# Where the selection rounds, the norm, the bias table and the clearing of S stand in a gated hybrid block

## The chip, the cores and the metric

The kernel runs on one core of a Trainium2 chip. The metric is device time in microseconds (us) of one execution. The kernel before takes 1400.65 us (median of three runs, 1398.86 to 1402.32).

Five instruction streams run side by side on the core: TensorE (PE, matrix multiplies), VectorE (DVE), ScalarE (ACT), GpSimd (POOL) and SyncE (SP, which issues the DMAs here). Each executes its own instructions in the order of the program and waits for the others by semaphores.

## The reference

One layer over 512 tokens of width 2048, in float32. `h = rmsnorm(x)` is projected by `w_in` into the inputs of two mixers, and the mixers are merged.

```python
proj = h @ w_in                      # a_q, a_f, a_i, a_g, c_q, c_kv, k_idx, w_idx, b_g, m_a, m_b
# A: HGRN2, 8 heads of 128
f = lb + (1 - lb) * sigmoid(a_f);  k = 1 - f
o = hgrn2_recurrence(silu(a_q) * 128**-0.5, k, log(f), a_i)
y_a = rmsnorm(o, gnorm) * silu(a_g)
# B: sparse attention, 8 heads; the indexer has 16 heads
score[t, s] = sum_h w_idx[t, h] * relu(q_idx[t, h] . k_idx[s])    # visible chunks only
top 128 keys of each token; softmax(q . k * 128**-0.5 + bias[t5_bucket(s - t)]) @ v
y_b = out * silu(b_g)
merged = sigmoid(m_a) * (y_a @ w_pa) + sigmoid(m_b) * (y_b @ w_pb)
return rmsnorm(x + merged @ w_out, final_norm_w)
```

## The kernel before

Every large product is made three times over, as high x high, high x low and low x high halves of a float32 (`mm3`, lines 75 to 78). A weight chunk is loaded (`wr`), rounded on ScalarE to its high half (`wh`, L72), and VectorE makes the rest (`wl`, L73). This is prepared two chunks ahead of the matmuls.

The program is a list of **jobs**, one after the other: the start; the plain and the "pair" projections; the **index stage** (eight jobs, two index heads each); the projections of the recurrences with the recurrences among them; the attention; the merge; the output. Nothing sorts the instructions: the order in which the code emits them is the order of each engine.

Work that is not a large product is spread among the matmuls by **lanes**. A lane is a queue of generators. Between groups of matmuls (12 of 384 columns in the index stage, 24 of 256 or 12 of 512 behind it) a job calls `pump()`, which issues waiting loads and stores and advances the first generator of every lane up to its next `yield`, in the order hgrn, top, att, norm, misc, t5. One such stretch is called a pump here; it takes TensorE some 3 to 4 us.

The lanes that matter here:

- **hgrn**: `hgrn_gen(p)`, the recurrence of heads 2p and 2p+1, run for p = 3, 2, 0, 1 one after the other. Its first pump loads a gate, clears `near` and `S` on GpSimd (L724, L725), and for p = 3 and 2 makes f, k and q (L730 to L732). Then eight levels, one a pump: TensorE makes the scores (`hl`, L81), VectorE scales q (L746, L753) and the totals (L758), GpSimd scales k (L755), VectorE merges the scores into `near` (L766) or copies them into `S` (L771, L775). The scores of a level need q and k of the level before. Then k is transposed (`hkt`), the states are made (`hp`) and the outputs (`ho`), their squares are summed (`hz`), ScalarE takes ln and exp (L821, L822), VectorE applies norm and gate (L825, L826) and splits the result (`hy`), which is stored to `ya_d`. The low half of the second head lies in the buffer of `S`, so the next clearing of `S` waits for that store.
- **top**: `top_gen`, 48 rounds (16 for each of three blocks of 256, 384 and 512 keys). A round finds the eight largest scores of each token (MAX8, L658) and strikes them out (MATCH_REPLACE, L659). One round a pump from the second job behind the index stage on; attention needs the end.
- **norm**: `norm_gen` normalises `ckv` for the keys and values (squares L575, sums `ns` on TensorE, ln and exp). **t5**: `t5_gen` makes the table of relative biases (matmuls L473 and L488, through a store and two loads). Both are queued by `open_branches`, at the head of the index stage.
- **misc**: in the index stage `idx_gen`, the scores `sc` of one head, their relu on ScalarE (L639) and the weighted sum on VectorE (L646).

Of the kernel before, what the change touches and what calls it, by code (L numbers as in the profile page):

```python
# [28 lines left out]
AF = mybir.ActivationFunctionType  # L29
OP = mybir.AluOpType  # L30
# [20 lines left out]
def hybrid_block(ctx, tc, x, norm_w, w_in, lb_table, gnorm_a, q_norm_w, kv_norm_w, w_uq,  # L51
# [3 lines left out]
    V, A, G, PE, SP = nc.vector, nc.scalar, nc.gpsimd, nc.tensor, nc.sync  # L55
# [12 lines left out]
    def bank(name):  # L68
        return sdp.tile([128, 512], F32, name=name, tag="sd")
# [19 lines left out]
    lb = const.tile([128, H], F32, name="lb")  # L89
    oml = const.tile([128, H], F32, name="oml")  # L90
    widx = const.tile([128, 4, 16], F32, name="widx")
    const.tile([128, 16], F32, name="gap")
    c_qw, c_kvw, c_iw, c_ib, c_gw = cols[:, 16:20], cols[:, 20:22], cols[:, 22:23], cols[:, 23:24], cols[:, 24:25]
# [19 lines left out]
    def leave(name):  # L113
        pools.pop(name)[0].__exit__(None, None, None)

    R = SimpleNamespace()


    specs = []
# [60 lines left out]
    lanes = {name: deque() for name in ("hgrn", "top", "att", "norm", "misc", "t5")}  # L180
# [255 lines left out]
    def open_branches():  # L436
        R.v = enter("values")
        R.s = enter("shared")
        R.q = enter("idx", side="right")
        R.M = R.s.tile([128, 1280], F32, name="M")  # L440
        R.ckh = R.s.tile([128, 2, T], FR, name="ckh")
        R.ckl = R.s.tile([128, 2, T], FR, name="ckl")
        R.ident = R.s.tile([128, 128], F32, name="ident")
        R.levels = R.s.tile([128, 6, 32], U8, name="levels")
        SP.dma_start(R.ident, c_ident)
        lev = R.q.tile([128, 6, 32], F32, name="lev", tag="bf")
        SP.dma_start(lev, c_levels.rearrange("p (l t) -> p l t", l=6))
        G.tensor_copy(R.levels, lev)
        R.i = enter("norms")
        R.ckv = R.i.tile([128, 2, T], F32, name="ckv")  # L450
        SP.dma_start(R.ckv, ckv_d.rearrange("f p t -> p f t"))
        for p in (3, 2):
            for n in "fkq":
                hg[p, n] = place(p, [128, 2, T], F32, "h" + n, "h" + n)
            for i, n in enumerate("qf"):
                SP.dma_start(hg[p, n], qf_d[i, 2 * p - 4:2 * p - 2].rearrange("f p t -> p f t"))
        lanes["norm"].append(norm_gen(R.ckv, 2, c_kvw, R.ckh, R.ckl))
        lanes["t5"].append(t5_gen())

    def t5_gen():  # L460
        rb = R.i.tile([128, H], F32, name="rb")
        oh = R.i.tile([128, 384], F32, name="oh")
        tl = R.i.tile([H, 384], F32, name="tl")
        flip = R.i.tile([128, 128], F32, name="flip")
        far = R.i.tile([H, 1], F32, name="far")
        G.memset(rb, 0.0)
        SP.dma_start(rb[0:32], rel_bias)
        SP.dma_start(oh, c_buckets)
        SP.dma_start(flip, c_flip)
        yield  # L470
        yield
        ps = bank("t5")
        PE.matmul(ps[:H, :384], rb, oh, start=True, stop=True)  # L473
        V.tensor_copy(far, ps[:H, 0:1])
        V.tensor_scalar(tl, ps[:H, :384], far, None, op0=OP.subtract)
        late[1].append(lambda: SP.dma_start(t5_d, tl))
        yield
        yield
        yield
        for h in range(0, H, 2):  # L480
            if h % 4 == 0:
                bf = R.i.tile([128, 4, 256], F32, name="bf")
                SP.dma_start(bf, bass.AP(tensor=t5_d.tensor, offset=t5_d.offset + h * 384,
                                         ap=[[1, 128], [384, 4], [1, 256]]))
                yield
                yield
            ps = bank("t5")
            PE.matmul(ps, flip, bf[:, h % 4:h % 4 + 2, :], start=True, stop=True)  # L488
            e = R.i.tile([128, 2, 256], F32, name="nt", bufs=2)
            V.tensor_copy(e, ps.rearrange("p (h c) -> p h c", h=2))  # L490
            late[1].append(lambda h=h, e=e: SP.dma_start(bh_d[h:h + 2].rearrange("h p c -> p h c"), e))
            yield
# [78 lines left out]
    def norm_gen(raw, n, w, hi, lo):  # L571
        ss = []
        for j in range(n):
            ss.append(R.i.tile([128, T], F32, name="nsq", bufs=2))
            A.activation(ss[j], raw[:, j, :], AF.Square)  # L575
            if j:
                V.tensor_add(ss[j], ss[j - 1], ss[j])
        yield
        sh = R.i.tile([128, T], FR, name="sumh")
        sl = R.i.tile([128, T], FR, name="suml")  # L580
        split(sh, sl, ss[-1])
        yield
        yield
        ps = bank("ns")
        mm(ps, ones_r, sh, True, False)
        mm(ps, ones_r, sl, False, True)
        r = rstd_row(ps, n * 128)
        yield
        for j in range(0, n, 2):
            ts = [R.i.tile([128, T], F32, name="nt", bufs=2) for _ in range(2)]  # L590
            for i, t in enumerate(ts):
                V.scalar_tensor_tensor(t, raw[:, j + i, :], w[:, j + i:j + i + 1], r, op0=OP.mult, op1=OP.mult)
            for i, t in enumerate(ts):
                split(hi[:, j + i, :], lo[:, j + i, :], t)
            yield
# [52 lines left out]


    def top_gen():  # L650
        V.memset(R.M[:, 0:128], 0.0)
        for b in range(4):
            V.memset(R.M[0:64, MO[b] + b * 128 + 64:MO[b] + b * 128 + 128], NEG)
        for b in (1, 2, 3):
            m = R.M[:, MO[b]:MO[b] + b * 128 + 128]
            for i in range(16):
                m8 = R.s.tile([128, 8], F32, name="m8", bufs=2)
                V.max(m8, m)  # L658
                V.match_replace(m, m8, m, GONE)  # L659
                if i == 15:  # L660
                    V.tensor_scalar(m, m, -2e38, NEG, op0=OP.is_gt, op1=OP.mult)
                yield


    def place(p, shape, dtype, name, tag):
# [30 lines left out]
    def af_evac(p):  # L696
        def evac(c, ps):
            if c == 0:
                hg[p, "f"] = place(p, [128, 2, T], F32, "hf", "hf")
                hg[p, "k"] = place(p, [128, 2, T], F32, "hk", "hk")  # L700
            f, k, h = hg[p, "f"][:, c, :], hg[p, "k"][:, c, :], 2 * p + c
            A.activation(f, ps, AF.Sigmoid)
            V.tensor_scalar(f, f, oml[:, h:h + 1], lb[:, h:h + 1], op0=OP.mult, op1=OP.add)
            V.tensor_scalar(k, f, -1.0, 1.0, op0=OP.mult, op1=OP.add)
        return evac

    def aq_evac(p):
        def evac(c, ps):
# [9 lines left out]
    def hgrn_gen(p):  # L718
# [3 lines left out]
        S = R.h.tile([128, 8, 128], F32, name="hS")  # L722
        near = R.h.tile([128, 8, 32], F32, name="hnear")
        G.memset(near, 0.0)  # L724
        G.memset(S, 0.0)  # L725
        qf, kf, tot = (a.rearrange("p c t -> p (c t)") for a in (q, k, f))
        if p >= 2:
            for c in range(2):
                h = 2 * p + c
                V.tensor_scalar(f[:, c], f[:, c], oml[:, h:h + 1], lb[:, h:h + 1], op0=OP.mult, op1=OP.add)  # L730
            V.tensor_scalar(k, f, -1.0, 1.0, op0=OP.mult, op1=OP.add)
            A.activation(q, q, AF.Copy, scale=128 ** -0.5)  # L732
        yield

        def scores(l, ps):
# [8 lines left out]
        def decay(l):  # L744
# [13 lines left out]
            V.tensor_tensor(nt, tv[:, :, 0], tv[:, :, 1], op=OP.mult)  # L758
            return nt

        for l in range(8):
            ps = bank("hl")
            scores(l, ps)
            tot = decay(l)
            if l < 6:
                V.copy_predicated(near, R.levels[:, l:l + 1, :].to_broadcast([128, 8, 32]),  # L766
                                  ps[:, 0:256].rearrange("p (n t) -> p n t", n=8))
            else:
                m = 1 << (l - 1)
                for h in range(0, 128, 2 * m):  # L770
                    V.tensor_copy(S[h:h + m, :, h + m:h + 2 * m],  # L771
                                  ps[h:h + m, 0:8 * m].rearrange("p (n t) -> p n t", n=8))
            if l == 6:
                for h in range(0, 128, 32):
                    V.tensor_copy(S[h:h + 32, :, h:h + 32], near[h:h + 32])  # L775
            yield

        kd = R.h.tile([128, 2, 3, 128], F32, name="hkd")
        for c in range(2):
            pt = bank("hkt")  # L780
# [36 lines left out]
        for c in range(2):  # L817
# [2 lines left out]
            mm(ps, ones_r, zs[c][1], False, True)  # L820
            A.activation(sq[:, c], ps, AF.Ln, bias=eps, scale=1.0 / 128)  # L821
        A.activation(sq, sq, AF.Exp, scale=-0.5)  # L822
        for c in range(2):
            r = sq[:, c]
            V.scalar_tensor_tensor(r, o[:, c], c_gw, r, op0=OP.mult, op1=OP.mult)  # L825
            V.tensor_tensor(r, r, gate[:, c], op=OP.mult)  # L826
# [316 lines left out]
    def end_index():  # L1143
        lanes["misc"].append(waiting.pop())
        drain("misc")
        leave("idx")
        leave("raws")
        R.h = enter("hgrn", side="right")
        lanes["hgrn"].extend((hgrn_gen(3), hgrn_gen(2)))

    def open_att():
        drain("norm")
# [353 lines left out]
```

## Time and profile before

| what | us |
|---|---|
| median of three runs | 1400.65 |
| the profiled execution, its own time | 1400.45 |
| its span in the trace | 1398.7 |
| PE busy in the span | 1361.7 (97%) |
| DVE busy | 1087.3 (78%) |
| ACT busy | 632.0 (45%) |
| POOL busy | 83.1 (6%) |

PE busy means that some matmul was in flight; TensorE at half its clock is busy as well, so the granted clock has to be read beside it. The idle time of the other engines matters only where TensorE waits for them.

### The profile page before, as it was taken

What the parts mean: (1) busy time and instruction counts of PE and PEld (TensorE: products, weight loads), DVE (VectorE), ACT (ScalarE), POOL (GpSimd) and SP (SyncE); (2) the same over time, 40 slices, a digit from 0 to 9 for tenths busy, and PEclk for the clock granted to TensorE, in tenths of its full rate; (3) what the DMA queues carried; (4) which work ended last, traced back from release to release, by engine and by line L of the source; (5) the groups of instructions that cost most, each with busy time, mean ns of one, the idle gap of its engine ahead of it and who ended that gap; (6) DMA issues with size and microseconds to landing.
All of it is one profiled execution on the core that took longest, in us unless ns stands there. A gap on an engine that the chain in (4) does not pass through costs nothing. (4 is left out here: it accounts for less than half of the span.)

```text
span 1398.7 us, 26795 instructions
## 1 busy us (share of the span) xinstructions
PE 1361.7 (97%) x10940; PEld 1258.8 (90%) x10940; DVE 1087.3 (78%) x1780; ACT 632.0 (45%) x1003; POOL 83.1 (6%) x85
## 2 busy tenths in 40 slices
PE   8999999999999999997998998999999999999997
PEld 7888999999999999996998787878888888899996
DVE  7786789988888888865786878795566658899856
ACT  6544544544544454435525241434534424454434
POOL 2100000000000000000030303031001100000000
PEclk9999999999999999998999999999999999999999
DMA  6345345544444544454422332334856556643464
GB/s 202 91 108 147 92 143 160 166 136 143 137 145 139 148 133 117 129 160 155 121 78 74 109 93 76 103 109 159 275 177 196 165 198 219 222 152 123 146 212 170
DMA packets 143598, 203.73 MB, mean 146 GB/s; under 512 B 10434, under 2 KB 84851, under 8 KB 143347
## 3 DMA queue, kind: packets, MB, share of 16 engines
q1 hardware_dynamic: 143186, 201.69, 46.3%
q8 instruction: 86, 1.41, 0.4%
q10 hardware_dynamic: 288, 0.33, 0.1%
q14 instruction: 38, 0.30, 0.1%
HBM read 166.84 MB, written 35.14 MB: 144 GB/s over the span
## 5 line engine op out<-in xcount | busy, mean ns | idle before, releaser
L150 ACT ACTIVATE bh<-wr 128x768 fp32r<-128x768 f32 x128 | 108.2, 845 | 221.5 <-issue 113.6
L152 ACT ACTIVATE wh<-sv 128x512 fp32r<-128x512 f32 x256 | 151.7, 623 | 83.9 <-DVE sv L145 64.9
L72 ACT ACTIVATE wh<-wr 128x1024 fp32r<-128x1024 f32 (+1 forms) x104 | 108.0, 1041 | 154.1 <-PE acc L77 56.0
L78 PE MATMUL pp<-sh,wl 128*128 128x256 f32 x624 | 172.8, 277 | 0.0
L76 PE MATMUL pp<-sh,wh 128*128 128x256 f32 x624 | 172.7, 277 | 0.0
L77 PE MATMUL pp<-sl,wh 128*128 128x256 f32 x624 | 172.7, 277 | 0.0
L73 DVE TENSOR_TENSOR wl<-wr,wh 128x1024 fp32r<-128x1024 f32 (+1 forms) x104 | 125.5, 1207 | 49.6 <-ACT wh L72 49.2
L153 DVE TENSOR_TENSOR bl<-wr,bh 128x768 fp32r<-128x768 f32 x128 | 122.3, 955 | 53.4 <-ACT bh L150 53.0
L154 DVE TENSOR_TENSOR wl<-sv,wh 128x1024 fp32r<-128x1024 f32 x128 | 156.5, 1223 | 7.4 <-ACT wh L152 1.1
L76 PE MATMUL acc<-xh,wh 128*128 128x512 f32 x304 | 123.1, 405 | 0.0
L78 PE MATMUL acc<-xh,wl 128*128 128x512 f32 x304 | 119.4, 393 | 0.0
L77 PE MATMUL acc<-xl,wh 128*128 128x512 f32 x304 | 119.2, 392 | 0.0
L77 PEld LDWEIGHTS pp<-sl,wh 128*128 128x128 f32 x624 | 117.3, 188 | 0.0
L78 PEld LDWEIGHTS pp<-sh,wl 128*128 128x128 f32 x624 | 117.3, 188 | 0.0
L76 PEld LDWEIGHTS pp<-sh,wh 128*128 128x128 f32 x624 | 117.3, 188 | 0.0
L76 PE MATMUL pp<-xh,bh 128*128 128x256 f32 x416 | 114.9, 276 | 0.0
L78 PE MATMUL pp<-xh,bl 128*128 128x256 f32 x416 | 114.9, 276 | 0.0
L77 PE MATMUL pp<-xl,bh 128*128 128x256 f32 x416 | 114.9, 276 | 0.0
L76 PE MATMUL acc<-yh,wh 128*128 128x512 f32 x256 | 100.2, 391 | 0.0
L77 PE MATMUL acc<-yl,wh 128*128 128x512 f32 x256 | 99.7, 390 | 0.0
L78 PE MATMUL acc<-yh,wl 128*128 128x512 f32 x256 | 99.7, 390 | 0.0
L145 DVE TENSOR_TENSOR sv<-wr 128x512 f32<-128x512 f32 x128 | 87.9, 686 | 8.5 <-DMA wr<-in_w_in_dram 4.9
(386 smaller groups left out, 3701.3 us busy)
## 6 DMA issues: line engine op xcount, KB each, us to landing
wr<-in_w_in_dram SPq DMA_DIRECT2D x136, 512.0 KB, 3.7
wr<-in_w_out_dram SPq DMA_DIRECT2D x32, 512.0 KB, 3.7
mg<-gate_d SPq DMA_DIRECT2D x48, 256.0 KB, 4.3
gate_d<-c SPq DMA_DIRECT2D x44, 256.0 KB, 4.6
wr<-in_w_in_dram SPq DMA_DIRECT2D x36, 256.0 KB, 3.1
wr<-in_w_pa_dram SPq DMA_DIRECT2D x16, 512.0 KB, 4.2
wr<-in_w_pb_dram SPq DMA_DIRECT2D x16, 512.0 KB, 5.0
x<-in_x_dram SPq DMA_DIRECT2D x8, 512.0 KB, 6.7
```

The lines of the kernel that those rows point to most:

```text
L72: A.activation(hi, src, AF.Copy)
L73: V.tensor_tensor(lo, src, hi.bitcast(F32), op=OP.subtract)
L76: PE.matmul(ps, lh, rh, start=first, stop=False, skip_group_check=True)
L77: PE.matmul(ps, lh, rl, start=False, stop=False, skip_group_check=True)
L78: PE.matmul(ps, ll, rh, start=False, stop=last, skip_group_check=True)
L145: V.tensor_tensor(sv[:, 0:2, :], b[:, 1:3, :], b[:, 0:1, :].to_broadcast([128, 2, 256]), op=OP.add)
L150: A.activation(bh, b[:, 1:4, :], AF.Copy)
L152: A.activation(vh[:, i:i + 2, :], sv[:, i:i + 2, :], AF.Copy)
L153: V.tensor_tensor(bl, b[:, 1:4, :], bh.bitcast(F32), op=OP.subtract)
L154: V.tensor_tensor(vl, sv, vh.bitcast(F32), op=OP.subtract)
```

## The change

- **Selection rounds.** `top_gen` no longer makes one round a pump. It collects credit: 0.55 a pump while a recurrence is in its eight levels (`R.hot`), 1.75 a pump otherwise, and makes a round for each whole credit.
- **Norm and bias table.** `norm_gen` and `t5_gen` are queued at the end of the index stage (`end_index`) instead of at its head.
- **f, k and q of p = 3 and 2** are made by `early_gen` during the index stage, in the hgrn lane. The affine forms f and k are two ScalarE activations (`forget`) instead of VectorE operations, for p = 0 and 1 too.
- **S** is cleared at level 4 instead of in the first pump, and the copies into it are made on ScalarE instead of VectorE.
- **A yield** stands between exp (L822) and the norm and gate (L825), so that a recurrence takes 17 pumps instead of 16.

```diff
--- before.py
+++ after.py
@@ -113,7 +113,7 @@
     def leave(name):
         pools.pop(name)[0].__exit__(None, None, None)
 
-    R = SimpleNamespace()
+    R = SimpleNamespace(hot=False)
 
 
     specs = []
@@ -454,8 +454,7 @@
                 hg[p, n] = place(p, [128, 2, T], F32, "h" + n, "h" + n)
             for i, n in enumerate("qf"):
                 SP.dma_start(hg[p, n], qf_d[i, 2 * p - 4:2 * p - 2].rearrange("f p t -> p f t"))
-        lanes["norm"].append(norm_gen(R.ckv, 2, c_kvw, R.ckh, R.ckl))
-        lanes["t5"].append(t5_gen())
+        lanes["hgrn"].append(early_gen())
 
     def t5_gen():
         rb = R.i.tile([128, H], F32, name="rb")
@@ -648,18 +647,23 @@
 
 
     def top_gen():
+
+        credit = 0.0
         V.memset(R.M[:, 0:128], 0.0)
         for b in range(4):
             V.memset(R.M[0:64, MO[b] + b * 128 + 64:MO[b] + b * 128 + 128], NEG)
         for b in (1, 2, 3):
             m = R.M[:, MO[b]:MO[b] + b * 128 + 128]
             for i in range(16):
+                while credit < 1:
+                    yield
+                    credit += 0.55 if R.hot else 1.75
+                credit -= 1
                 m8 = R.s.tile([128, 8], F32, name="m8", bufs=2)
                 V.max(m8, m)
                 V.match_replace(m, m8, m, GONE)
                 if i == 15:
                     V.tensor_scalar(m, m, -2e38, NEG, op0=OP.is_gt, op1=OP.mult)
-                yield
 
 
     def place(p, shape, dtype, name, tag):
@@ -698,11 +702,25 @@
             if c == 0:
                 hg[p, "f"] = place(p, [128, 2, T], F32, "hf", "hf")
                 hg[p, "k"] = place(p, [128, 2, T], F32, "hk", "hk")
-            f, k, h = hg[p, "f"][:, c, :], hg[p, "k"][:, c, :], 2 * p + c
-            A.activation(f, ps, AF.Sigmoid)
-            V.tensor_scalar(f, f, oml[:, h:h + 1], lb[:, h:h + 1], op0=OP.mult, op1=OP.add)
-            V.tensor_scalar(k, f, -1.0, 1.0, op0=OP.mult, op1=OP.add)
+            A.activation(hg[p, "f"][:, c, :], ps, AF.Sigmoid)
+            forget(p, c)
         return evac
+
+    def forget(p, c):
+        f, k, h = hg[p, "f"][:, c, :], hg[p, "k"][:, c, :], 2 * p + c
+        A.activation(f, f, AF.Identity, bias=lb[:, h:h + 1], scale=oml[:, h:h + 1])
+        A.activation(k, f, AF.Copy, bias=1.0, scale=-1.0)
+
+    def early_gen():
+        for p in (3, 2):
+            for _ in range(3):
+                yield
+            forget(p, 0)
+            yield
+            forget(p, 1)
+            yield
+            A.activation(hg[p, "q"], hg[p, "q"], AF.Copy, scale=128 ** -0.5)
+            yield
 
     def aq_evac(p):
         def evac(c, ps):
@@ -722,14 +740,7 @@
         S = R.h.tile([128, 8, 128], F32, name="hS")
         near = R.h.tile([128, 8, 32], F32, name="hnear")
         G.memset(near, 0.0)
-        G.memset(S, 0.0)
         qf, kf, tot = (a.rearrange("p c t -> p (c t)") for a in (q, k, f))
-        if p >= 2:
-            for c in range(2):
-                h = 2 * p + c
-                V.tensor_scalar(f[:, c], f[:, c], oml[:, h:h + 1], lb[:, h:h + 1], op0=OP.mult, op1=OP.add)
-            V.tensor_scalar(k, f, -1.0, 1.0, op0=OP.mult, op1=OP.add)
-            A.activation(q, q, AF.Copy, scale=128 ** -0.5)
         yield
 
         def scores(l, ps):
@@ -758,7 +769,10 @@
             V.tensor_tensor(nt, tv[:, :, 0], tv[:, :, 1], op=OP.mult)
             return nt
 
+        R.hot = True
         for l in range(8):
+            if l == 4:
+                G.memset(S, 0.0)
             ps = bank("hl")
             scores(l, ps)
             tot = decay(l)
@@ -768,13 +782,14 @@
             else:
                 m = 1 << (l - 1)
                 for h in range(0, 128, 2 * m):
-                    V.tensor_copy(S[h:h + m, :, h + m:h + 2 * m],
-                                  ps[h:h + m, 0:8 * m].rearrange("p (n t) -> p n t", n=8))
+                    A.activation(S[h:h + m, :, h + m:h + 2 * m],
+                                 ps[h:h + m, 0:8 * m].rearrange("p (n t) -> p n t", n=8), AF.Copy)
             if l == 6:
                 for h in range(0, 128, 32):
-                    V.tensor_copy(S[h:h + 32, :, h:h + 32], near[h:h + 32])
+                    A.activation(S[h:h + 32, :, h:h + 32], near[h:h + 32], AF.Copy)
             yield
 
+        R.hot = False
         kd = R.h.tile([128, 2, 3, 128], F32, name="hkd")
         for c in range(2):
             pt = bank("hkt")
@@ -820,6 +835,7 @@
             mm(ps, ones_r, zs[c][1], False, True)
             A.activation(sq[:, c], ps, AF.Ln, bias=eps, scale=1.0 / 128)
         A.activation(sq, sq, AF.Exp, scale=-0.5)
+        yield
         for c in range(2):
             r = sq[:, c]
             V.scalar_tensor_tensor(r, o[:, c], c_gw, r, op0=OP.mult, op1=OP.mult)
@@ -1147,6 +1163,8 @@
         leave("raws")
         R.h = enter("hgrn", side="right")
         lanes["hgrn"].extend((hgrn_gen(3), hgrn_gen(2)))
+        lanes["norm"].append(norm_gen(R.ckv, 2, c_kvw, R.ckh, R.ckl))
+        lanes["t5"].append(t5_gen())
 
     def open_att():
         drain("norm")
```

ScalarE at the head of the index stage (`qih` and `relu` belong to the index heads, `nsq`, `sumh` to the norm). Before:

```order
L72 ACTIVATE qih<-acc 128x384
L575 ACTIVATE nsq<-ckv 128x512 x2
L72 ACTIVATE qih<-acc 128x384
L72 ACTIVATE sumh<-nsq 128x512
L639 ACTIVATE relu<-sc 128x512
L639 ACTIVATE relu<-sc 128x384
L639 ACTIVATE relu<-sc 128x256
L72 ACTIVATE wh<-wr 128x1024
L72 ACTIVATE qih<-acc 128x384
```

Now, five rows further on:

```order
L72 ACTIVATE qih<-acc 128x384
L638 ACTIVATE relu<-sc 128x512
L638 ACTIVATE relu<-sc 128x384
L638 ACTIVATE relu<-sc 128x256
L72 ACTIVATE qih<-acc 128x384
L711 ACTIVATE hf<-hf,lb,oml 128x512
L712 ACTIVATE hk<-hf 128x512
L638 ACTIVATE relu<-sc 128x512
L638 ACTIVATE relu<-sc 128x384
L638 ACTIVATE relu<-sc 128x256
```

The squares and the split of the norm have left; forget's two activations stand between two index heads, one pair a pump in two pumps and the copy of q in the third, for p = 3 and again for p = 2.

VectorE from the end of the second recurrence (p = 2) to the first level of the third (p = 0); `hy` is the split of the result, L746, now L757, the first scaling of q. Before, from the last operation of the gate on:

```order
L826 TENSOR_TENSOR hk<-hk,hg 128x512
L658 MAX m_9724<-M 128x8
L659 MATCH_REPLACE M<-m_9724,M 128x384
L713 SCALAR_TENSOR_TENSOR hq<-acc,hq 128x512
L73 TENSOR_TENSOR hy_9742<-hk,hy_9741 128x512
L73 TENSOR_TENSOR hy_9746<-hk,hy_9745 128x512
L658 MAX m_9749<-M 128x8
L659 MATCH_REPLACE M<-m_9749,M 128x384
L73 TENSOR_TENSOR wl<-wr,wh 128x1024
L658 MAX m_9790<-M 128x8
L659 MATCH_REPLACE M<-m_9790,M 128x384
L746 TENSOR_TENSOR hq<-hq,hf 128x1024
```

Now, from the second of two rounds behind the gate on:

```order
L664 MATCH_REPLACE M<-m_9799,M 128x384
L666 TENSOR_SCALAR M<-M 128x384
L73 TENSOR_TENSOR hy_9828<-hk,hy_9827 128x512
L73 TENSOR_TENSOR hy_9832<-hk,hy_9831 128x512
L663 MAX m_9835<-M 128x8
L664 MATCH_REPLACE M<-m_9835,M 128x512
L663 MAX m_9838<-M 128x8
L664 MATCH_REPLACE M<-m_9838,M 128x512
L73 TENSOR_TENSOR wl<-wr,wh 128x1024
L663 MAX m_9876<-M 128x8
L664 MATCH_REPLACE M<-m_9876,M 128x512
L757 TENSOR_TENSOR hq<-hq,hf 128x1024
```

Between gate and first scaling there were three rounds of 384 keys and the q of the projection (L713); now there are two of 384 keys with their closing comparison and three of 512, and L713 lies further up.

GpSimd in the third recurrence. Before:

```order
L724 MEMSET hnear 128x256
L725 MEMSET hS 128x1024
L755 TENSOR_TENSOR hk<-hk,hf 128x512
L755 TENSOR_TENSOR hk<-hk,tot_9924 128x256x2
L755 TENSOR_TENSOR hk<-hk,tot_9989 128x128x4
L755 TENSOR_TENSOR hk<-hk,tot_10060 128x64x8
```

Now:

```order
L742 MEMSET hnear 128x256
L766 TENSOR_TENSOR hk<-hk,hf 128x512
L766 TENSOR_TENSOR hk<-hk,tot_10010 128x256x2
L766 TENSOR_TENSOR hk<-hk,tot_10075 128x128x4
L775 MEMSET hS 128x1024
L766 TENSOR_TENSOR hk<-hk,tot_10143 128x64x8
```

The clearing of `S` stood ahead of all scalings of k and now stands behind the third.

## Rows read from the trace of the kernel before

**Rows 1.** The page: its span and the line of TensorE in part 1

```profile
span 1398.7 us, 26795 instructions
...
PE 1361.7 (97%) x10940; PEld 1258.8 (90%) x10940; DVE 1087.3 (78%) x1780; ACT 632.0 (45%) x1003; POOL 83.1 (6%) x85
```

**Rows 2.** PE's waits, 600:1120: line, releaser, us in total, times, longest

```profile
PE hl L81 <- POOL hk L755: 4.4, 2, 4.2
PE hl L81 <- DVE hk L731: 3.8, 1, 3.8
PE hl L81 <- DVE hq L746: 3.8, 2, 2.3
PE sc L76 <- ACT qih L72: 3.7, 2, 2.5
PE t L473 <- DMA oh<-in_buckets_dram: 2.4, 1, 2.4
...
PE hl L81 <- DVE hq L713: 1.4, 2, 0.8
```

**Rows 3.** Windows, index stage: busy us by engine, then PEclk, DMA share, GB/s

```profile
632.00:642.00 10.00, 5.20 (x20) 3.67 (x18) 5.58 (x10) 5.77 (x12) 0.39 (x2) 0.73 0.94 314
642.00:652.00 10.00, 9.93 (x40) 8.15 (x40) 1.86 (x5) 4.56 (x6) 0.00 (x0) 0.76 0.14 48
660.00:700.00 40.00, 40.00 (x217) 36.66 (x217) 31.40 (x52) 22.99 (x47) 0.51 (x2) 1.00 0.42 119
```

**Rows 4.** PE's timeline, index stage: start us, us, what, idle before

```profile
631.50 0.34 PE L76 MATMUL acc<-cqh,wh 128*128 128x384 f32 x1
...
695.66 0.33 PE L76 MATMUL acc<-cqh,wh 128*128 128x384 f32 x1
...
699.34 0.39 PE L76 MATMUL sc<-kih,qih 128*128 128x512 f32 x1
...
700.91 0.28 PE L76 MATMUL acc<-wh,xh 128*128 128x256 f32 x1
```

**Rows 5.** ScalarE's timeline at the head of the index stage

```profile
634.61 1.15 ACT L575 ACTIVATE nsq<-ckv 128x512 f32<-128x512 f32 x2 [5.73 <-DMA ckv<-ckv_d]
```

**Rows 6.** Windows where the second and third recurrences begin

```profile
764.00:768.00 4.00, 0.23 (x16) 0.23 (x18) 3.92 (x9) 2.44 (x3) 0.00 (x0) 0.79 0.19 26
768.00:774.00 6.00, 6.00 (x104) 4.66 (x101) 4.04 (x8) 0.00 (x0) 0.00 (x0) 0.57 0.99 329
828.00:848.00 20.00, 12.89 (x256) 12.23 (x253) 14.92 (x29) 2.79 (x3) 3.82 (x3) 0.83 0.43 134
```

**Rows 7.** PE's timeline where the third recurrence begins

```profile
819.14 0.40 PE L81 MATMUL hz<-hzl,ones_r 128*128 128x512 f32 x1
...
827.87 0.46 PE L81 MATMUL hl<-hq,hk 128*32 128x32 f32 x32
...
834.67 1.08 PE L81 MATMUL hl<-hq,hk 128*32 128x32 f32 x64 [2.31 <-DVE hq L746]
```

**Rows 8.** GpSimd's timeline, third recurrence

```profile
841.51 0.95 POOL L725 MEMSET hS<- 128x1024 f32 x1 [43.02 <-DMA ya_d<-hy]
```

**Rows 9.** VectorE by line and shape, 690:960: count, busy us, mean ns

```profile
L658 DVE MAX8 m<-M 128x8 f32<-128x512 f32 x16 | 11.0, 689 | 0.2
...
L659 DVE MATCH_REPLACE8 M<-m,M 128x512 f32<-128x512 f32 x16 | 10.8, 677 | 0.0
...
L658 DVE MAX8 m<-M 128x8 f32<-128x384 f32 x16 | 8.8, 553 | 0.1
```

**Rows 10.** PE by line, 620:960: the bias table's matmuls

```profile
L488 PE MATMUL t<-bf,flip 128*128 128x512 f32 x8 | 4.1, 592 | 0.0
...
L473 PE MATMUL t<-oh,rb 128*8 128x384 f32 x2 | 1.4, 823 | 2.4 <-DMA oh<-in_buckets_dram 2.4
```

**Rows 11.** ScalarE by line and shape, 690:960

```profile
L810 ACT ACTIVATE ho<-ho 128x512 f32<-128x512 f32 x7 | 4.2, 599 | 20.7 <-PE ho L81 20.7
...
L919 ACT ACTIVATE P<-P,mx 128x512 f32<-128x512 f32 x1 | 0.7, 722 | 3.3 <-DVE mx L914 3.3
```

## The prediction

> **What bounds the kernel now.** TensorE does: the page gives it 97% of the span [rows 1]. So I looked for where it stands still or runs slowly. The list of PE's waits was read first: between 600 and 1120 us TensorE waits 13.4 us in the recurrences' levels (4.4 + 3.8 + 3.8 + 1.4), all for q or k from VectorE or GpSimd, and in the index stage for rounded index queries (3.7) and for the bias table's input (2.4) [rows 2]. Second, the windows, for the granted clock: in 632:652 it is 0.73 and 0.76, in 764:774 it is 0.79 and 0.57, in 828:848 it is 0.83 [rows 3, 6]. [...] Third, the timelines, for how long the same work takes undisturbed. Behind the third recurrence TensorE has no wait of weight up to the output, so what is saved ahead of that moves the end.
>
> **Index stage, norm and bias table.** At the head of the stage ScalarE stands 5.73 us at the norm's squares, because ckv has not landed [rows 5], and the index queries queue behind it; then TensorE waits for the bias table's input, and part of this runs at half clock. From 631.50, where the second job begins, to 700.91, where the next stage begins, are 69.4 us [rows 4]. In it stand 14 pairs of projection and head scores and one more block of scores. Undisturbed, a pair takes 699.34 - 695.66 = 3.68 us and the last block 700.91 - 699.34 = 1.57 us [rows 4]: 14 x 3.68 + 1.57 = 53.1 us. The stage gets 16.3 us shorter.
>
> Of that, matmuls that only move come back behind it: the four of the table 4.1 us, its first one 0.7 us (1.4 us here, at half clock), both [rows 10], and two of the norm, about 0.5 us: 5.3 us. They are a net loss nowhere else: the table's input is now asked for two pumps ahead, without the 2 MB of f and q loads in front of it.
>
> In their place ScalarE gets forget's two activations in four pumps and the copy of q in two. The stage's steady part keeps ScalarE 22.99 of 40 us busy [rows 3], 2.1 us of a pair's 3.68. Two activations of 512 columns add 1.2 us (599 ns each) to 1.4 us (722 ns, the form with an operand from memory) [rows 11]: 3.3 to 3.5 us, still under 3.68. The first one waits for the loads of f, which come behind ckv; its fourth pump should be late enough. I take 0.5 us of wait, between 0 and the 2.5 us of the longest wait for qih [rows 2].
>
> [...]
>
> **The recurrences' starts.** f, k and q of the second recurrence are ready long before; its wait for L731, 3.8 us, goes. `S` is cleared at level 4, behind the first scalings of k. Before, the clearing stood first and itself stood until the store of the last result had landed (841.51, idle 43.02 us) [rows 8]; the wait for POOL of 4.2 us [rows 2] goes. The two for q (3.8 and 1.4 us) came from VectorE's rounds. All of them: 13.4 us. With them goes the half clock: 764:774 has (4 x 0.21 + 6 x 0.43) x 2 = 6.8 us of it, TensorE idle in the first 1.5 us, so 2.6 us lost; 828:848 has 20 x 0.17 x 2 = 6.8 us, two falls, 3.4 us lost [rows 6]. Together 6.0 us.
>
> **What is late next.** (a) The third recurrence's level 1. Its q was 2.31 us late [rows 7]. Behind the norm and gate VectorE now has two rounds of 384 keys and three of 512 ahead of q, where it had three of 384 and the q of the projection. A round of 384 is 2 x 0.55 = 1.1 us, one of 512 is 0.69 + 0.68 = 1.37 us [rows 9]; with 0.5 us for the closing comparison and 0.6 less for the projection's q this is 3 x 1.37 + 0.5 - 1.1 - 0.6 = 2.9 us more. TensorE comes later too: by the pump of the new yield, (827.87 - 819.37) / 3 = 2.83 us [rows 7], less the 0.6 us that it stood just ahead (the other one of L713's two) [rows 2]. The wait: 2.31 + 2.9 - 2.2 = 3.0 us. Such a wait has let the clock fall, at 1.7 us (each fall in 828:848) to 2.6 us; I take 2.2. So 5.2 us, between 0 and 8.
>
> (b) The second recurrence's level 1. Its five rounds there are of 256 keys and smaller, and the same pump is gained: 0.4 us, between 0 and the 3.0 us of (a).
>
> (c) The fourth: the mask and bias sums of the attention stand on GpSimd ahead of its level 4. They cost the last 0.3 us of POOL's 4.4 [rows 2]; the clearing, 0.95 us [rows 8], now queues directly behind them and ahead of k: 1.2 us.
>
> (d) In the first recurrence norm and table share the levels, where there were no rounds: VectorE gets some 6 us in eight pumps, less the copies into S. Nothing, with the lookahead of two chunks as cover.
>
> The fourth recurrence meets no rounds, since credit ends them some eight pumps earlier: 48 = 0.55 x 16 + 1.75 x 22. ScalarE's copies into `S` are hidden: it is idle there, and `ho` needs them four pumps later.
>
> **The sum**, against the profiled execution's own 1400.45 us (span 1398.7 [rows 1] and 1.75 us around it; the median of the runs is 1400.65): -16.3 + 5.3 + 0.5 - 13.4 - 6.0 + 5.2 + 0.4 + 1.2 = -23.1, so 1377.3 us.
>
> **Rivals.**
> - *No level waits any more*: the rounds overlap better than (a) reckons. For it: in the steady levels VectorE kept up with one round a pump. Against: the 2.31 us were waited for behind the same gate. Without (a) and (b): 1371.7 us. Chance 0.20.
> - *The clock falls in the index stage all the same.* A wait of 1.2 us for qih stands right ahead of the second job and stays (3.7 in two, longest 2.5 [rows 2]). The fall was 10 x (0.27 + 0.24) x 2 = 10.2 us long [rows 3]; at half clock that is 5.1 us: 1382.4 us. Against: the clock fell after the 2.5 us wait, not after this one. Chance 0.13.
> - *The rounds starve the recurrences' tails.* 1.75 rounds are 1.9 to 2.4 us a pump; with half a weight chunk, the squares' split, norm and gate VectorE is about full there. If it falls behind a pump's length, `ho` or `hz` waits in three recurrences, 2.5 us and a fall of 1.7 each: 12.6 us, 1390 us. Chance 0.10; a milder form at 1396 to 1405 has 0.03.
> - *Slower: VectorE bounds the pumps without levels.* Same place, but every pump lasts as long as VectorE's work, not only the starts. 27 pumps take 1.75 rounds or belong to such tails. It decides the sign if VectorE has 1.0 us more a pump than TensorE (27 x 1.0 beats 23.1 + 4); by the rows it has about as much as TensorE, so it would need rounds half again as long as shown. At 1.2 us a pump: +32.4 - 23.1, 1410 us. Chance 0.04.
>
> My forecast itself has 0.50, its own range 1373 to 1382. About 0.3%, 4.2 us, can be told from no change. Faster: 0.50 + 0.20 + 0.13 + 0.10 = 0.93; within 0.3%: 0.03; slower: 0.04. The range 1369 to 1388 leaves out the starved tails and the slower cases above, and holds the case without waits below.
>
> **What the changed kernel's profile would show.** Right: the index stage from its second job to the next stage in about 53 us at full clock; no wait for oh or L731; no wait for POOL of 4 us, but one of about 1 us in the fourth recurrence; one wait for q (L757) of about 3 us in the third, with a fall of the clock. Wrong: waits of `ho` or `hz` for VectorE, of the table's matmuls for their loads, of `acc` for weights, or a granted clock under 1 in the index stage.

## The result, and the profile after

The changed kernel takes 1380.30 us (median of four runs, 1379.72 to 1381.59) against 1400.53 us before: 0.9857 of the time, 95% interval 0.9840 to 0.9874, 20.2 us less. The forecast was 1377.3 us, its range 1369 to 1388. The profiled execution took 1379.72 us, 20.7 us less than the profiled one of before, where the sum had 23.1.

The page after, where [rows 1] stood before:

```profile
span 1377.9 us, 26785 instructions
...
PE 1353.1 (98%) x10940; PEld 1253.3 (91%) x10940; DVE 1072.2 (78%) x1738; ACT 654.3 (47%) x1047; POOL 83.0 (6%) x85
```

TensorE is still the bound. It is busy 8.6 us less than before, though it does the same 10940 matmuls: less of the span lies at half clock (the mean granted clock is 0.996, before 0.990). Half clock is a granted clock of 0.50: in windows of 0.5 us both traces have 1.00 or 0.50, and values between them only where it changes. The other 12 us are waits. TensorE's waits, 600 to 1120 us, the view of [rows 2] (line, releaser, us in total, times, longest):

```profile
PE hl L81 <- DVE hq L757: 6.2, 2, 5.3
PE sc L76 <- ACT qih L72: 1.2, 1, 1.2
PE hl L81 <- POOL hk L766: 1.1, 1, 1.1
PE hl L81 <- DVE tot L769: 1.0, 1, 1.0
PE sc L78 <- DVE qil L73: 0.6, 1, 0.6
```

The waits for L731, for the table's input and for relu are gone; `hq L757`, the scaling of q, is the line that was L746. The wait for relu is a line of the same list of before that [rows 2] leaves out:

```profile
PE sc L76 <- ACT relu L639: 2.0, 2, 1.9
```

What is new is one long wait for q, 5.3 us, and one of 1.0 us for the totals.

The index stage: the windows that in [rows 3] had clocks of 0.73 and 0.76 (0.50 from 637 to 646.5 us), and the timeline of [rows 4]:

```profile
632.00:642.00 10.00, 10.00 (x59) 9.60 (x58) 6.08 (x11) 6.68 (x13) 0.34 (x1) 1.00 1.00 347
642.00:652.00 10.00, 10.00 (x59) 9.70 (x59) 8.72 (x14) 8.09 (x18) 0.00 (x0) 1.00 0.28 93
```

```profile
631.33 0.33 PE L76 MATMUL acc<-cqh,wh 128*128 128x384 f32 x1
...
684.33 0.28 PE L76 MATMUL acc<-wh,xh 128*128 128x256 f32 x1
```

From its second job to the next stage are 53.0 us, at full clock, TensorE without a pause.

The third recurrence: TensorE's timeline (as [rows 7]) and two windows, in its wait and behind it:

```profile
817.65 0.76 PE L81 MATMUL hl<-hq,hk 128*32 128x32 f32 x64
...
826.66 1.08 PE L81 MATMUL hl<-hq,hk 128*32 128x32 f32 x64 [5.31 <-DVE hq L757]
```

```profile
821.40:826.60 5.20, 0.00 (x0) 0.00 (x0) 5.10 (x10) 0.00 (x0) 0.00 (x0) 0.73 0.25 54
826.60:832.00 5.40, 5.34 (x88) 5.16 (x88) 5.37 (x10) 0.00 (x0) 1.50 (x1) 0.63 1.01 336
```

TensorE stood from 821.35 to 826.66, and of the 5.4 us behind it 5.4 x 0.37 x 2 = 4.0 us were at half clock (the granted clock is 0.50 from 824 to 830.5 us): 2.0 us lost. Before, two falls, 0.83 on average from 828 to 848 us, cost 3.4 us here [rows 6].

GpSimd in the fourth recurrence:

```profile
910.03 3.62 POOL L904 TENSOR_TENSOR MB<-M,bh 128x256 f32<-128x256 f32 x3
913.58 0.95 POOL L775 MEMSET hS<- 128x1024 f32 x1
914.49 1.09 POOL L766 TENSOR_TENSOR hk<-hk,tot 128x512 f32<-128x512 f32 x1
```

The clearing queues behind the attention's sums and ahead of k, and TensorE waits 1.1 us for that k.

### The profile page after: what moved, and what is told of

It is laid out like the page before. It is cut to its first block, busy times and chain, and to the rows that moved or that the text cites. A ratio compares the mean times of both kernels' runs of the same rounds, so it can differ in the third digit from the quotient of the medians.

```text
span 1377.9 us, 26785 instructions
## 1 busy us (share of the span) xinstructions
PE 1353.1 (98%) x10940; PEld 1253.3 (91%) x10940; DVE 1072.2 (78%) x1738; ACT 654.3 (47%) x1047; POOL 83.0 (6%) x85
```

## The experiments

The ratio beside each time is to runs of the kernel before on the same chip. Those had medians of 1400.65 us (the first four experiments), 1399.58 us (affine forms, extra yield, only the norm and the table, three rates) and 1399.32 us (only the early f, k and q; the norm in two pumps). The changed kernel was not run again beside the experiments, so a difference of 1 us from it, or between two kernels on different chips, says nothing by itself. Where parts of a time are named, they are read from the profiled execution.

**The norm and the table back at the head.**

```diff
 def open_branches():
     lanes["hgrn"].append(early_gen())
+    lanes["norm"].append(norm_gen(R.ckv, 2, c_kvw, R.ckh, R.ckl))
+    lanes["t5"].append(t5_gen())
 def end_index():
     lanes["hgrn"].extend((hgrn_gen(3), hgrn_gen(2)))
-    lanes["norm"].append(norm_gen(R.ckv, 2, c_kvw, R.ckh, R.ckl))
-    lanes["t5"].append(t5_gen())
```

> The changed kernel with the norm and the bias table queued at the head of the index stage again. Theory A (the move is what shortened the index stage): the stage takes its 16.4 us again (69.4 us from its second job), the moved matmuls (about 5.5 us) and the wait of 1.0 us in the first recurrence go, so 1379.8 + 16.4 - 6.5 = about 1389.7 us, 1387 to 1392, with ScalarE standing at the norm's squares for ckv and a stretch at half clock. Theory B (what helped was that the loads stood before a shorter queue of other work; forget's activations in the stage cover the wait): under 1384 us.

1391.35 us (0.9938 of before, 0.9924 to 0.9951), 11.1 us more than the changed kernel: theory A. The stage takes 69.5 us again (632.08 to 701.55). Two of TensorE's waits and ScalarE's wait at the norm's squares:

```profile
PE t L474 <- DMA oh<-in_buckets_dram: 3.6, 1, 3.6
PE sc L76 <- ACT relu L640: 3.4, 3, 1.9
```

```profile
633.18 1.15 ACT L576 ACTIVATE nsq<-ckv 128x512 f32<-128x512 f32 x2 [4.67 <-DMA ckv<-ckv_d]
```

They answer to [rows 2] with the wait for relu of before, and to [rows 5]. The stretch from the first to the second recurrence also gives the price of the moved matmuls: 60.23 us without them (707.10 to 767.33), 66.40 us with them, of which 1.02 us is the wait for the totals, so 5.15 us.

**One round in every pump.**

```diff
-                    credit += 0.55 if R.hot else 1.75
+                    credit += 1.0
```

> The changed kernel with one selection round in each pump (credit 1.0 everywhere). Theory A (the credit's 1.75 rounds outside the levels put five rounds ahead of q in the third recurrence and made its wait of 5.3 us; in the levels VectorE keeps up with one round a pump, as before): q waits for 1 to 2 us in the third recurrence and not at all in the second, some 1 us comes in the fourth, where rounds now meet the levels: 1375 to 1378 us. Theory B (the credit is what took the waits for q out of the levels, 3.8 and 1.4 us before): these come back with a fall of the clock, and the time is 1383 to 1387 us.

1379.47 us (0.9853, 0.9839 to 0.9866): no difference from the changed kernel that can be told. Theory A had the mechanism, and was 1.5 us too low. The waits for q:

```profile
PE hl L81 <- DVE hq L757: 4.4, 2, 2.8
...
PE hl L81 <- DVE hq L764: 0.8, 2, 0.5
```

The 4.4 us are 1.6 us in the third recurrence, as theory A had it, and 2.8 us in the fourth, where it had reckoned 1 us; the mean granted clock of this execution is 0.993, the changed kernel's 0.996. So the credit as it stands wins nothing: it takes the rounds out of the fourth recurrence's start and puts as much in front of the third's.

**S cleared in the first pump again.**

```diff
         G.memset(near, 0.0)
+        G.memset(S, 0.0)
...
-            if l == 4:
-                G.memset(S, 0.0)
```

> The changed kernel with S cleared in the first pump again. Theory A (the prediction's term): GpSimd stands at the clearing until the store of the last result has landed, the third recurrence waits for k 4 us and the clock falls once more: 1379.8 + 4.2 + 1.7 - 1.1 = about 1384.6 us. Theory B (the extra pump and the 5.3 us wait for q already cover the store: it is issued at 825.1 to 827.8 and takes about 5.5 us, so the clearing ends near 834.3 and k near 835.8, when its level starts at about 835.6; the fourth recurrence loses its wait of 1.1 us): 1378 to 1380 us.

1394.64 us (0.9959, 0.9947 to 0.9972), 14.3 us more. Both theories were wrong: B in the sign (it put the start of level 2 at 835.6, where it is 832.0 in the changed kernel, and so saw cover where there was none), A in the size. TensorE's wait for k, and GpSimd's timeline at the clearings of the second and third recurrence:

```profile
PE hl L81 <- POOL hk L767: 11.1, 3, 6.6
```

```profile
768.51 0.95 POOL L743 MEMSET hS<- 128x1024 f32 x1 [46.56 <-DMA ya_d<-hy]
...
842.71 0.95 POOL L743 MEMSET hS<- 128x1024 f32 x1 [48.75 <-DMA ya_d<-hy]
```

In the third recurrence 4.2 us are waited, as in the kernel before. But the second waits 6.6 us, and the clock falls with it (0.72 from 764 to 776 us), where in the kernel before no wait for GpSimd stood at all: there the wait for L731 had let the store land, as the run with only the early f, k and q shows below.

**Few rounds from the gate on.**

```diff
         A.activation(sq, sq, AF.Exp, scale=-0.5)
         yield
+        R.hot = True
```

> The changed kernel with the low credit (0.55 a pump) from the norm and gate on, through the first pump of the next recurrence, not only in the levels. Between gate and the first scaling of q stand one round in the third recurrence and two in the second, where five stood; the rounds still end before the fourth. Theory A (these rounds make q late): no wait for q in the second and third recurrence and no fall of the clock there, 5.3 + 0.9 + 2.0 = 8.2 us less: 1371.6 us, 1370.5 to 1373. Theory B (q is late because of the weight chunk's split and the gate that wait for ScalarE, and the rounds fill a time that was idle anyway): 1377 to 1380 us.

1375.49 us (0.9823, 0.9810 to 0.9837), 4.8 us less than the changed kernel. The waits for q:

```profile
PE hl L81 <- DVE hq L757: 1.3, 1, 1.3
...
PE hl L81 <- DVE hq L764: 0.9, 2, 0.5
```

The waits at the starts of the second and third recurrence are gone, as theory A has it, and the mean granted clock of the five runs is 0.995 to 0.999, where the four of the changed kernel had 0.993 to 0.996; the 1.3 us are in the fourth, since the last rounds now run up to it. The median is 3.9 us above A's 1371.6, the profiled execution (1376.28 us) 4.7; of these, 1.3 are that wait, 1.6 a fall of the clock at the head of the index stage (last section), 0.9 the later levels (L764), and 0.9 stay open.

**Affine forms and copies on VectorE.**

```diff
-        A.activation(f, f, AF.Identity, bias=lb[:, h:h + 1], scale=oml[:, h:h + 1])
-        A.activation(k, f, AF.Copy, bias=1.0, scale=-1.0)
+        V.tensor_scalar(f, f, oml[:, h:h + 1], lb[:, h:h + 1], op0=OP.mult, op1=OP.add)
+        V.tensor_scalar(k, f, -1.0, 1.0, op0=OP.mult, op1=OP.add)
...
-                    A.activation(S[h:h + m, :, h + m:h + 2 * m], ps[...], AF.Copy)
+                    V.tensor_copy(S[h:h + m, :, h + m:h + 2 * m], ps[...])
...
```

> The changed kernel with forget's two affine forms and the copies into S on VectorE again, everything else as changed. Theory A (no engine but TensorE bounds the places where they stand: in the steady index stage VectorE is busy 30.3 and ScalarE 24.6 of 40 us, in the last levels VectorE meets 0.55 rounds a pump): no difference, 1379 to 1381.5 us. Theory B (moving them to ScalarE is what keeps VectorE in time): waits for VectorE in the last levels or in the index stage, 1383 us or more.

1380.94 us (0.9864, 0.9850 to 0.9877): no difference. The two forms in the index stage, by line and shape, in the changed kernel and then in this one:

```profile
L711 ACT ACTIVATE hf<-hf,lb,oml 128x512 f32<-128x512 f32 x4 | 3.3, 813 | 0.0
L712 ACT ACTIVATE hk<-hf 128x512 f32<-128x512 f32 x4 | 2.5, 632 | 0.1
```

```profile
L711 DVE TENSOR_SCALAR hf<-hf,oml,lb 128x512 f32<-128x512 f32 x4 | 2.2, 539 | 0.0
L712 DVE TENSOR_SCALAR hk<-hf 128x512 f32<-128x512 f32 x4 | 1.7, 427 | 0.1
```

VectorE does the pair in 0.97 us, ScalarE in 1.45 us, and it costs nothing on either: TensorE waits for neither there.

**Without the extra yield.**

```diff
         A.activation(sq, sq, AF.Exp, scale=-0.5)
-        yield
```

> The changed kernel without the extra yield between exp and the norm and gate. Theory A (the pump gained was mostly lost: a weight chunk's split, and the wait for ScalarE's rounding of it, now stand ahead of the gate, so the gate begins 4.5 us ahead of level 0 in place of 3.6; nearly as many rounds follow): q waits about 6.2 us in the third recurrence and about 1.8 in the second, 1381 to 1383 us. Theory B (the pump counts whole, 2.8 us, as the prediction had it): q waits about 8 us in the third and 3.5 us in the second with a fall of the clock there, 1386 us or more.

1388.81 us (0.9921, 0.9907 to 0.9934), 8.5 us more. Theory B had the time and the second recurrence, where q waits 3.3 us and the clock falls; it had the third wrong, where q waits 5.2 us, no more than with the yield. Theory A had neither. A wait that no theory had appears in a tail:

```profile
PE hl L81 <- DVE hq L757: 8.5, 2, 5.2
PE acc L78 <- DVE wl L73: 2.2, 1, 2.2
...
PE hl L81 <- DVE hq L731: 0.6, 1, 0.6
```

Behind the 3.3 us and behind the 2.2 us the granted clock is 0.83 for a window of 10 us each (760 to 770, 890 to 900), which is 1.7 us lost each time. With 2.4 us more for q in the second recurrence, the 2.2 us and the 0.6 us these falls make 8.6 of the 9.1 us between the profiled executions.

VectorE at the gate and at the scaling of q in the third recurrence:

```profile
813.11 0.75 DVE L840 SCALAR_TENSOR_TENSOR hk<-ho,cols,hk 128x512 f32<-128x512 f32 x1 [3.30 <-ACT hk L837]
...
825.10 1.22 DVE L757 TENSOR_TENSOR hq<-hq,hf 128x1024 f32<-128x1024 f32 x1
```

Without the yield the norm and gate wait for exp with nothing useful ahead of them, and the weight chunk's split comes after them: that is how the 2.2 us for `wl` at 890 us come about (VectorE stands 5.9 us before the gate there). In the third recurrence the gate begins 3.6 us ahead of level 0 (816.68), 0.9 less than with the yield; but TensorE is held by L731 there and comes 0.8 us later, so q is waited for no longer. So the rival of the starved tails names a mechanism that exists; the yield keeps it away.

**Only the norm and the table moved, in the kernel before.** The first diff above turned round, in the kernel before.

> The kernel before with nothing changed but the norm and the bias table queued behind the index stage. Theory A (this move alone makes the index stage short): the stage falls from 69.4 to 53 us, the moved matmuls cost about 5.5 us and the norm's VectorE work about 1 us in the first recurrence: 1389 to 1392 us. Theory B (the early forms of f and k, which this kernel leaves at the recurrences' starts, and the norm meet on VectorE in the first recurrence and give much of it back): 1393 us or more.

1390.78 us (0.9936, 0.9922 to 0.9950), 8.8 us less than before: theory A. The stage falls to 53.0 us. Of the shortened stage something is lost again in the third recurrence, where the wait for k grows from 4.2 to 5.6 us:

```profile
PE hl L81 <- POOL hk L753: 7.2, 3, 5.6
PE hl L81 <- DVE hk L729: 3.7, 1, 3.7
```

**Only the early f, k and q, in the kernel before.**

```diff
         lanes["t5"].append(t5_gen())
+        lanes["hgrn"].append(early_gen())
...
-        if p >= 2:
-            for c in range(2):
-                h = 2 * p + c
-                V.tensor_scalar(f[:, c], f[:, c], oml[:, h:h + 1], lb[:, h:h + 1], op0=OP.mult, op1=OP.add)
-            V.tensor_scalar(k, f, -1.0, 1.0, op0=OP.mult, op1=OP.add)
-            A.activation(q, q, AF.Copy, scale=128 ** -0.5)
```

> The kernel before with one part of the change: f, k and q of p = 3 and 2 are made during the index stage, the affine forms on ScalarE. Theory A (the wait for L731 and the half clock behind it, 3.8 + 2.6 us, covered the clearing of S, which in the kernel before ended at 775.8 us; without them the second recurrence waits for the same clearing instead): a wait for GpSimd of 5 to 6.5 us stands where L731 was waited for, and the time is 1398 to 1401 us, no change. Theory B (the parts add up, as the prediction's sum has it): 1400.2 - 3.8 - 2.6 = about 1394 us.

1405.08 us (1.0042, 1.0028 to 1.0055): slower by 5.8 us. Theory A's mechanism, with a time still worse than it had. TensorE's wait, and GpSimd at the clearing in the second recurrence:

```profile
PE hl L81 <- POOL hk L766: 10.3, 3, 6.2
```

```profile
777.30 0.95 POOL L742 MEMSET hS<- 128x1024 f32 x1 [40.54 <-DMA ya_d<-hy]
```

The wait for L731 (3.8 us) is gone, and 6.2 us for k stand in its place, waiting for the store: 2.4 us more. The index stage is longer too in the profiled execution, 73.6 us from its first scores (629.14) to the next stage (702.75) where before it had 72.0 (628.93 to 700.91); the mean granted clock of the execution is 0.988, before 0.990.

**Three rates, and the clearing one level earlier.**

```diff
-    R = SimpleNamespace(hot=False)
+    R = SimpleNamespace(hot=False, rate=1.8)
...
-                    credit += 0.55 if R.hot else 1.75
+                    credit += R.rate
...
-        R.hot = True
+        R.hot, R.rate = True, 0.85
         for l in range(8):
-            if l == 4:
+            if l == 3:
...
-        R.hot = False
+        R.hot, R.rate = False, 1.8
...
         A.activation(sq, sq, AF.Exp, scale=-0.5)
         yield
+        R.rate = 0.3
```

> The changed kernel with three rates: 0.3 rounds a pump from the norm and gate to the next recurrence's levels, 0.85 in the levels, 1.8 elsewhere, so that one round stands between gate and q where five stood, and the rounds end before the norm and gate of the third recurrence; and S cleared at level 3 in place of 4, ahead of the attention's mask and bias sums. Theory A (rounds behind the gate make q late; at under one round a pump the levels don't wait): against the changed kernel the 5.3 + 2.0 us of the third recurrence, 0.9 of the second and 1.1 of the fourth go: 1371 us, 1370 to 1373. Theory B (the low credit in the levels was needed): waits for q or the totals in the levels give it back, 1376 us or more.

1373.84 us (0.9815, 0.9801 to 0.9828), 6.5 us less than the changed kernel. What is left of the waits in the levels:

```profile
PE hl L81 <- DVE hq L764: 1.1, 3, 0.5
PE hl L81 <- DVE tot L769: 1.0, 1, 1.0
...
PE hl L81 <- POOL hk L766: 0.3, 1, 0.3
```

No start of a recurrence waits for the first scaling of q. The granted clock is 1.00 from 824 to 834 us, where the changed kernel had 0.66 from 822 to 832. Theory A: the waits that it named are gone, and the 0.85 rounds cost the levels only the 1.1 us for L764. The time is 0.8 us above its range; in the profiled execution the index stage lost 1.5 us to a fall of the clock (last section).

**The same, with the norm in two pumps.**

```diff
             V.scalar_tensor_tensor(t, raw[:, j + i, :], w[:, j + i:j + i + 1], r, ...)
+            yield
             for i, t in enumerate(ts):
                 split(hi[:, j + i, :], lo[:, j + i, :], t)
```

> The kernel with three rates and the clearing at level 3, and one yield more in the norm, so that its scaling and its split fall into two pumps of the first recurrence. Theory A (the wait of 1.0 us for the totals in the first recurrence comes from the 3.7 us that VectorE gives the norm in one pump): the wait goes, about 1 us less, 1372 to 1374 us against 1373.8. Theory B (the wait is the scaling's alone): the wait stays, or moves to the pump behind.

1372.75 us (0.9810, 0.9797 to 0.9824), the fastest of all; 1.1 us from the one above, which by the times alone can't be told from none. The wait for the totals says it:

```profile
PE hl L81 <- DVE tot L770: 0.3, 1, 0.3
```

0.3 us in place of 1.0: theory A for the most part. Between the two profiled executions are 2.25 us (1374.15 and 1371.90): 0.7 are this wait, and 1.5 the fall of the clock in the index stage, which this one did not have. So the yield is worth about 0.7 us.

## Why the prediction was right, point by point

- **Index stage**, -16.3 us: 53.0 us where 53.1 was reckoned from undisturbed pairs. Putting the norm and table back at the head brings the stage to 69.5 us again, and moving them alone is enough for 53.0. The cause is shown; how much of it is the norm's and how much the table's no run separates.
- **Moved matmuls**, +5.3: 5.15 by the run with the norm at the head.
- **Early ScalarE waits**, +0.5: none. Only the 1.2 us for qih of before stands in the list. The pair of activations was reckoned at 1.2 to 1.4 us from [rows 11]; it takes 0.813 + 0.632 = 1.45 us, 0.18 us more for the form with two pointer operands than for the one with none. VectorE makes the first in 0.54 us, ScalarE in 0.81; but the run with these forms on VectorE shows that here the price decides nothing.
- **The level waits**, -13.4, **and their half clock**, -6.0: they went, but the parts were put down wrongly. The prediction gave 3.8 + 2.6 us to the early f, k and q, and 4.2 + 1.7 to the late clearing, as if each would bring its own. Alone, the early forms make the kernel 5.8 us slower and win nothing: the wait for L731 had covered the store that the clearing waits for, and the wait that takes its place is 2.4 us longer (of the rest, 1.6 us are the index stage's in the profiled execution). Taking back the clearing alone costs 14.3 us. The sum was right because both were made. This was a weakness of its working that the result doesn't show. The factor 2 in the terms for half clock is measured: before, the granted clock is 0.50 from 766.5 to 773 us, from 835 to 837.5 and from 845 to 848.
- **(a) The third recurrence's level 1**, 5.2 us reckoned, 5.3 + 2.0 = 7.3 measured. This is the term that was mis-sized. VectorE at the gate and at the scaling of q, before and then after:

```profile
824.30 0.75 DVE L825 SCALAR_TENSOR_TENSOR hk<-ho,cols,hk 128x512 f32<-128x512 f32 x1 [4.33 <-ACT hk L822]
...
833.40 1.22 DVE L746 TENSOR_TENSOR hq<-hq,hf 128x1024 f32<-128x1024 f32 x1
```

```profile
812.06 1.23 DVE L73 TENSOR_TENSOR wl<-wr,wh 128x1024 fp32r<-128x1024 f32 x1 [2.46 <-ACT wh L72]
813.20 0.75 DVE L841 SCALAR_TENSOR_TENSOR hk<-ho,cols,hk 128x512 f32<-128x512 f32 x1
...
825.39 1.22 DVE L757 TENSOR_TENSOR hq<-hq,hf 128x1024 f32<-128x1024 f32 x1
```

From gate to scaling are 9.1 us before and 12.2 after: 3.1 more, 2.9 reckoned. But the prediction let TensorE come later by the whole pump of the new yield, 2.83 us. The gate began 827.87 - 824.30 = 3.57 us ahead of level 0 before [rows 7], and 817.65 - 813.20 = 4.45 us after: 0.9 us were gained. The rest went into the weight chunk's split at 812.06, which stands ahead of the gate since the yield, and for which VectorE waits 2.5 us until ScalarE, behind exp, has rounded the chunk. TensorE, no longer held by L713, reached level 1 0.8 us sooner (0.6 reckoned): 2.31 + 3.1 - 0.9 + 0.8 = 5.3 us. That the rounds make q late is shown by the runs with fewer of them behind the gate, in which the wait goes; that the yield gains this start nothing, by the run without it, which waits 5.2 us in the same place: the 0.9 us that it brings the gate forward go into the 0.8 us by which TensorE comes sooner.
- **(b)** 0.4 reckoned, 0.85 measured; here the yield does count, since without it the wait is 3.3 us. **(c)** 1.2 reckoned, 1.1 measured; at level 3, ahead of the sums, the clearing leaves 0.3. **(d)** nothing reckoned, 1.0 measured: the lookahead doesn't cover the totals, which the next level's k needs at once, and the norm in two pumps takes most of it away.

With these sizes the sum is 1377.3 - 0.5 + 2.1 + 0.45 - 0.1 + 1.0 = 1380.3 us; the profiled execution had 1379.7.

Of the rivals, *no level waits any more* fell by the 5.3 us. *The clock falls in the index stage* did not happen in the profiled execution (1.00 from 632 to 652 us) but does in others (0.83 from 626 to 636 us with the forms on VectorE), and costs 1.5 us where 5.1 were reckoned (last section). *The starved tails* come without the yield. *VectorE bounds the pumps* did not show: between the levels of the second and third recurrence TensorE was busy 25.00 of 25.00 us (790 to 815).

## What to carry to other kernels

Where two waits end at nearly the same time, taking the earlier one away uncovers the other: price the parts of such a change together, and ask of each wait that goes what had time to finish in it. An instruction put off by one step gains that step only if nothing waits in the place that it now takes; look at what its engine does first there. Background work shared out by a rate belongs where nothing on the same engine is due: the few steps between one recurrence's last operation and the next one's first want almost none of it.

## What was not expected of the hardware

The same instructions with the same two waits at the head of the index stage (1.24 and 0.62 us) brought a fall of the clock in some kernels' profiles and none in others. Window 626 to 636, the changed kernel and then the one with the affine forms on VectorE, which differs nowhere ahead of it:

```profile
626.00:636.00 10.00, 8.14 (x45) 7.21 (x44) 6.09 (x10) 7.06 (x14) 0.34 (x1) 1.00 0.92 290
```

```profile
626.00:636.00 10.00, 8.12 (x36) 7.18 (x35) 5.19 (x8) 6.07 (x12) 0.60 (x1) 0.83 0.98 315
```

It fell there in six of the ten experiments. Its price is read from the stage's first scores, where the first of the two waits ends, to the next stage. The changed kernel (to 684.33, above), and then the one with the forms on VectorE:

```profile
628.74 0.50 PE L76 MATMUL sc<-kih,qih 128*128 128x512 f32 x1 [1.24 <-ACT qih L72]
```

```profile
628.31 0.50 PE L76 MATMUL sc<-kih,qih 128*128 128x512 f32 x1 [1.25 <-ACT qih L72]
...
685.45 0.28 PE L76 MATMUL acc<-wh,xh 128*128 128x256 f32 x1
```

These are 55.6 and 57.1 us. All four kernels with the fall that have the norm behind the stage take 57.1 to 57.2 us, and all with the norm there and without the fall 55.6: 1.5 to 1.6 us each time. The runs of the changed kernel and of each experiment spread by 0.9 to 2.4 us; that this fall is a part of it is likely but not shown, since only one execution of each kernel has a trace. What decides whether the clock falls there, no run shows.
